# A hybrid decoder block on one core: retention's decay moved into its keys, and the norm work of the heads moved from GpSimd to ScalarE and VectorE

## The chip, the cores and the metric

The kernel runs on one core of one Trainium2 chip. The time is device microseconds of one launch. The core has TensorE (matmuls and transposes), VectorE, ScalarE and GpSimd (elementwise work), and SyncE, whose queue issues nearly all of this kernel's DMAs. In the profile's rows they are PE (PEld is its weight load), DVE, ACT, POOL and SP.

## The reference, cut to what matters

One layer, 512 tokens, model width 1024, everything in float32:

```
h = RMSNorm(x) ;  [q_r,k_r,v_r,g_r, q_f,k_f,v_f,f_f, a_r,a_f] = h @ W_in
y_r = W_ro( silu(g_r) * GroupNorm(Retention(rot(q_r), rot(k_r)/8, v_r)) * g_ret_norm )
y_f = W_fo( ForgettingAttention(RMSNorm(q_f)*g_fox_q, RMSNorm(k_f)*g_fox_k, v_f, log sigmoid(f_f + b)) )
x = x + W_out( sigmoid(a_r)*y_r + sigmoid(a_f)*y_f ) ;  x = x + SwiGLU(RMSNorm(x))

# Retention, 4 heads, keys of 64, values of 128, in chunks of 128 tokens; lg = log of the head's decay
decay[i,j] = exp((i-j)*lg) for i >= j, else 0
out_i   = sum_j (q_i . k_j) decay[i,j] v_j  +  exp((i+1)*lg) * (q_i @ state)
state'  = exp(128*lg) * state + sum_j exp((127-j)*lg) k_j^T v_j
# GroupNorm: per token and head over the 128 values: (o - mean) * rsqrt(var + EPS) * g_ret_norm
```

Forgetting attention has 8 heads of 64; its queries and keys are normed per token and head over their 64 columns.

## The kernel before, in words

Products of float32 are made of three matmuls in the float32r type: a high part (a ScalarE cast, tiles wh, xh) and a low part (a VectorE subtraction, wl, xl) of each operand, high by high, low by high, high by low (`three`, line 179). Weights come in units of 128x1024 (`load_w`, line 152: a DMA into tile raw), are cast on ScalarE (line 162) and subtracted on VectorE (line 163), so each unit needs both engines before TensorE can use it. A 128x512 matmul of these is the kernel's main instruction.

The work goes in stages: the combined projection (first the columns of q_r and k_r into rz, then k, v and gates of retention through sums of blocks of the weights, up to about 62 us), then retention interleaved with the projections of q_f, k_f, v_f and the gates a_r, a_f; then forgetting attention interleaved with the remaining gates and y_r; then the output product, SwiGLU and its down product. The change touches the second stage.

What sets the order: TensorE's order is written out by hand. While `pinned[0]` is true each matmul is chained behind the one before it, and `fill(us)` puts so many microseconds of projection matmuls between the pieces of retention. The order of the DMAs of SyncE (`move`) is chained in the same way. On the other engines a planner orders instructions by when they are ready in its own model, and the code's order breaks ties; `after(a, b)` ties single ones on the same engine. So an instruction may run long before one that the code issues ahead of it.

Retention works chunk by chunk, t from 0 to 3 (loop at line 868):

- `ret_rotate(t)` (line 504), on GpSimd: seven instructions. Products of the two halves of rz with cosine and sine (ta, tb, then tcc, td, 256 columns each), a difference and a sum into rot, and kz, the keys multiplied by their head's zeta = exp((127-j)*lg). For chunk 0 the first of them waits for `last_low`, a VectorE subtraction at the end of the first stage (line 514).
- `ret_square(t)` (line 528): VectorE transposes 32x32 blocks of rot, four DMAs write them to memory; `ret_get(t)` reads them back as rT, with columns along partitions; `ret_keys(t)` copies the keys' half on ScalarE into rK (line 544); `ret_decay(t)` multiplies the queries' half by exp((i+1)*lg) into rX on VectorE (line 549).
- `ret_scores(t)` (line 553): scores on TensorE into two banks tp, multiplied by the decay factors on VectorE into sT (line 561); then kz by values into a bank, and the new state sn (lines 570, 574).
- `ret_values(t)` (line 577): sT by values, and from chunk 1 on rX by state, into two banks sc.
- `ret_norm(t)` (line 590): per head statistics (line 597), a reciprocal root in steps on 128x4 (tiles n4v, n4y, n4a, lines 124 to 132), then og (line 605), all VectorE.
- `ret_out(t)` (line 608): GpSimd multiplies the gate gs by g_ret_norm (line 610); VectorE multiplies og by it (line 611); TensorE transposes og (line 85) into a bank tp; a cast on ScalarE and a subtraction on VectorE (lines 188, 189) make orh and orl.

The projection of q_f has its evacuation in `evac_qf` (line 650: ScalarE for the columns, and in the second half VectorE for the forget gate fz, line 654), that of k_f in `evac_kf`. Behind each evacuated block of tokens `head_norm` squares on ScalarE (line 634) and sums per head on VectorE (line 635); behind the last, a reciprocal root on 128x32 (n8v, n8y, n8a) and then GpSimd multiplies all four blocks by it (line 641), and q_f also by the norm weights (line 643). `turn_heads` transposes 32x32 blocks on VectorE (line 675), and DMAs through memory put heads' columns along partitions, where `fox_prep` (line 700) makes the parts of queries and keys. `turn_q` (line 689) is called twice a chunk and does one step of this for q_f at a time.

Of the kernel before, what the change touches and what calls it, by code (L numbers as in the profile page):

```python
# [17 lines left out]
P = 128  # L18
# [19 lines left out]
C_EARLY = C_GCH + 2  # L38
# [14 lines left out]
def block_kernel(ctx: ExitStack, tc, x, xT, c_early, c_tab, c_late, w_qf, w_tok, w_vg, w_a, w_y, w_o, w_gu, w_gl, w_dn, w_dh, out):  # L53
# [64 lines left out]
    def rsqrt(dst, ss, inv_n, shape, nm, pool=None, behind=None):  # L118
# [5 lines left out]
        first = ts(out=v, in0=ss, scalar1=inv_n, scalar2=EPS, op0=ALU.mult, op1=ALU.add)  # L124
# [210 lines left out]
    def split_to_parts(src, h, l):  # L335
        nc.scalar.copy(out=h, in_=src)
        tt(out=l, in0=src, in1=f32(h), op=ALU.subtract)
# [166 lines left out]
    def ret_rotate(t):  # L504
        z5 = rz[:, t, :].rearrange("p (a h s d) -> p a h s d", a=2, h=RH, s=2)
        z1, z2 = z5[:, :, :, 0, :], z5[:, :, :, 1, :]
        c = cosv[:, t].broadcast_to([P, 2, RH, 32])
        s = sinv[:, t].broadcast_to([P, 2, RH, 32])
        rot = rwk.tile([P, 512], F32, name="rot", tag="rot", bufs=3)
        r5 = rot.rearrange("p (a h s d) -> p a h s d", a=2, h=RH, s=2)  # L510
        ta = rwk.tile([P, 2, RH, 32], F32, name="ta", tag="ta", bufs=1)
        tb = rwk.tile([P, 2, RH, 32], F32, name="tb", tag="tb", bufs=1)
        first = gp.tensor_tensor(out=ta, in0=z1, in1=c, op=ALU.mult)
        if t == 0:
            tc.add_manual_dep(first.ins, last_low.ins.name, mybir.DependencyInfo(mybir.DependencyClass.Sync, mybir.DependencyReason.DATA), reason="GpSimd's part comes behind most of the sums")
        gp.tensor_tensor(out=tb, in0=z2, in1=s, op=ALU.mult)
        gp.tensor_tensor(out=r5[:, :, :, 0, :], in0=ta, in1=tb, op=ALU.subtract)
        td = rwk.tile([P, 2, RH, 32], F32, name="td", tag="ta", bufs=1)
        tcc = rwk.tile([P, 2, RH, 32], F32, name="tcc", tag="tb", bufs=1)
        gp.tensor_tensor(out=tcc, in0=z1, in1=s, op=ALU.mult)  # L520
        gp.tensor_tensor(out=td, in0=z2, in1=c, op=ALU.mult)
        gp.tensor_tensor(out=r5[:, :, :, 1, :], in0=tcc, in1=td, op=ALU.add)
        kz = rwk.tile([P, 256], F32, name="kz", tag="kz", bufs=3)
        last = gp.tensor_tensor(out=kz.rearrange("p (h d) -> p h d", h=RH), in0=rot[:, 256:512].rearrange("p (h d) -> p h d", h=RH),
                         in1=ce[:, C_ZETA:C_ZETA + RH].rearrange("p (h o) -> p h o", o=1).broadcast_to([P, RH, RDK]), op=ALU.mult)
        ret[t].update(rot=rot, kz=kz, rotated=last)
# [15 lines left out]
    def ret_keys(t):  # L542
        rK = rwk.tile([P, 2, P], F32, name="rK", tag="rK")
        nc.scalar.copy(out=rK.rearrange("p a (c i) -> p a c i", i=32), in_=ret[t]["rT"][:, :, 2:4, :].rearrange("p c a i -> p a c i"))
        ret[t].update(rK=rK)

    def ret_decay(t):
        rX = rwk.tile([P, 2, P], F32, name="rX", tag="rX")
        ret[t]["decay"] = tt(out=rX.rearrange("p a (c i) -> p a c i", i=32), in0=ret[t]["rT"][:, :, 0:2, :].rearrange("p c a i -> p a c i"),
           in1=xiT.rearrange("p a (c i) -> p a c i", i=32), op=ALU.mult)  # L550
        ret[t].update(rX=rX)

    def ret_scores(t):
        rT, kz = ret[t]["rT"], ret[t]["kz"]
        sT = rwk.tile([P, 512], F32, name="sT", tag="sT")
        sps = [bank("tp") for e in range(2)]
        for e, sp in enumerate(sps):
            rows = slice(e * 64, (e + 1) * 64)
            for a in range(2):
                mm(sp[:, a * P:(a + 1) * P], lhsT=ret[t]["rK"][rows, a, :], rhs=rT[rows, :, a, :], start=True, stop=True)  # L560
            tt(out=sT[:, e * 256:(e + 1) * 256], in0=sp[:, 0:256], in1=dec[:, e * 256:(e + 1) * 256], op=ALU.mult)
        ret[t].update(sT=sT)
        if t < NT - 1:
# [12 lines left out]

    def ret_values(t):
        rT, sT = ret[t]["rT"], ret[t]["sT"]
# [5 lines left out]
        if t:  # L584
            for e, a, os in pairs:
                rows = slice(e * 64, (e + 1) * 64)
                mm(o[e][:, os], lhsT=ret[t]["rX"][rows, a, :], rhs=ret[t]["st"][rows, a, :], start=False, stop=True, skip_group_check=True)
        ret[t].update(o=o)

    def ret_norm(t):  # L590
# [10 lines left out]
        rsqrt(r4, mv[:, :, 1], 1.0, [P, RH], "n4")  # L601
# [6 lines left out]
    def ret_out(t):  # L608
        og = ret[t]["og"]
        after(gp.tensor_tensor(out=gs[:, t, :], in0=gs[:, t, :], in1=gret, op=ALU.mult), ret[2]["rotated"])  # L610
# [5 lines left out]
        ret[t]["split"] = split_ps(pt.rearrange("p (h q) -> p h q", h=RH), orh[:, :, tq], orl[:, :, tq])  # L616
# [9 lines left out]
    gp.tensor_tensor(out=gqk, in0=gqk, in1=cl[:, C_GQK + FD:C_LATE], op=ALU.mult)  # L626

    def head_norm(z, g=None):
# [3 lines left out]
        def one(t):  # L632
# [3 lines left out]
            if t == NT - 1:  # L636
                r8 = sm.tile([P, NT, FH], F32, name="r8", tag="r8")
                rsqrt(r8.rearrange("p t h -> p (t h)"), s8.rearrange("p t h -> p (t h)"), 1.0 / FD, [P, NT * FH], "n8", behind=ret[0].get("normed"))
                for u in range(NT):
                    z3 = z[:, u, :].rearrange("p (h d) -> p h d", h=FH)  # L640
                    gp.tensor_tensor(out=z3, in0=z3, in1=r8[:, u, :].rearrange("p (h o) -> p h o", o=1).broadcast_to([P, FH, FD]), op=ALU.mult)
                    if g is not None:
                        gp.tensor_tensor(out=z3, in0=z3, in1=g.rearrange("p (o d) -> p o d", o=1).broadcast_to([P, FH, FD]), op=ALU.mult)
                normed.append(z)
# [3 lines left out]
    qnorm, knorm = head_norm(qf, gqk), head_norm(kf)  # L648

    def evac_qf(t, c, acc):  # L650
        sc = rstd1[:, t:t + 1]
        act(out=qf[:, t, c * 256:c * 256 + 256], in_=acc[:, 0:256], func=AF.Copy, scale=sc)
        if c:
            fox["fz"] = stt(out=fz[:, t, :], in0=acc[:, 256:264], scalar=sc, in1=ce[:, C_BF:C_BF + FH], op0=ALU.mult, op1=ALU.add)  # L654
            qnorm(t)

    def evac_kf(t, c, acc):
        act(out=kf[:, t, :], in_=acc, func=AF.Copy, scale=rstd1[:, t:t + 1])
        knorm(t)
# [10 lines left out]
    def turn_heads(z, ts_=range(NT)):  # L670
# [189 lines left out]
    move(rd1, rt)  # L860
    ret_rotate(2)
# [4 lines left out]
    ret_decay(0)  # L866
    ret_square(1)
    for t in range(NT):
        if t == 1:
            ret_rotate(t + 2)  # L870
# [13 lines left out]
        if t + 1 < NT:  # L884
            ret_decay(t + 1)
# [587 lines left out]
def _constants():  # L1473
# [8 lines left out]
    def rope(a):  # L1482
        a = a.astype(f).reshape(NT, P, half).transpose(1, 0, 2)
        return np.stack([a, a * f(RDK ** -0.5)], 2).reshape(P, NT * 2 * half)

    diff = idx[None, :] - idx[:, None]
    dec = [np.where(diff >= 0, ex(np.maximum(diff, 0) * lg[h]), 0).astype(f) for h in range(RH)]
    xi = np.stack([np.concatenate([np.tile(ex((idx + f(1)) * lg[2 * a + e]), (RDK, 1)) for e in range(2)]) for a in range(2)], 1).reshape(P, 2 * P)
    zeta = np.stack([ex((f(P - 1) - idx) * lg[h]) for h in range(RH)], 1)
    gch = ex(f(P) * lg)  # L1490
# [4 lines left out]
        "ident": np.eye(P, dtype=f), "xi": xi, "zeta": zeta, "gch": gchp, "tri": tri, "mask": mask,  # L1495
        "cos": rope(np.cos(ang)), "sin": rope(np.sin(ang)), "dec": np.concatenate([dec[0], dec[2], dec[1], dec[3]], 1),
# [7 lines left out]
def _layout(i):  # L1504
# [5 lines left out]
        _CONST["zeta"], _CONST["gch"]], 1)  # L1510
# [63 lines left out]
```

## Time and profile before

| | |
|---|---|
| median of 3 runs | 689.62 us (687.66, 689.62 and 1730.48) |
| profiled execution, own time | 689.82 us |
| its span, first to last instruction | 688.0 us |
| TensorE busy | 674.8 us (98%) |
| VectorE busy | 541.3 us (79%) |
| ScalarE busy | 350.5 us (51%) |
| GpSimd busy | 76.3 us (11%) |
| granted TensorE clock, mean | 0.997 |

A row of a timeline gives start, duration, engine, line, operation, tile written, tiles read, shapes and count; in brackets stands the idle time before it on its engine and what ended that. A matmul's duration is modelled to its end and overlaps the next one: the pace is read from the starts. A row by group gives busy time, mean nanoseconds of one, and the idle time before. Lines are those of the kernel; 82 and 85 are the helpers for all matmuls and all transposes, so tiles tell them apart. In the rows of forgetting attention, pT is its transposed weights.

### The profile page before, as it was taken

How to read it: one execution, taken by the hardware profiler on the slowest of the kernel's cores; microseconds unless marked ns; L12 is line 12 of the kernel's file. 1: busy time of each engine (PE TensorE's matmuls, PEld its weight loads, DVE VectorE, ACT ScalarE, POOL GpSimd, SP SyncE). 2: the span in 40 equal slices, each digit the busy share in tenths (PEclk: the TensorE clock that was granted, in tenths of full speed). 3: DMA queues.
4: the chain of work that ended last, by engine and by line, in shares of the span. 5: the costliest groups of instructions: out<-in, count | busy, mean ns of one | idle time of the engine just before them, and what ended most of it. 6: DMA issues, size and time to landing. Idle time of an engine off the chain costs nothing.

```text
span 688.0 us, 9396 instructions
## 1 busy us (share of the span) xinstructions
PE 674.8 (98%) x3375; PEld 562.8 (82%) x3375; DVE 541.3 (79%) x869; ACT 350.5 (51%) x515; POOL 76.3 (11%) x97
## 2 busy tenths in 40 slices
PE   8999998999999999999999999999999999999998
PEld 6877976888887777788888888888888898888997
DVE  6899489875768684576979998989989888756794
ACT  6667353431546444554656655564646474443341
POOL 0013946010212210000230000000000000000000
PEclk9999999999999999999999999999999999999999
DMA  8910543525638878526710614536362522644221
GB/s 271 421 51 32 153 141 93 193 84 185 199 96 243 221 224 255 175 92 236 283 61 1 244 32 146 150 113 183 86 180 52 124 101 61 160 143 159 81 103 62
DMA packets 85806, 101.30 MB, mean 147 GB/s; under 512 B 52960, under 2 KB 62336, under 8 KB 84992
## 3 DMA queue, kind: packets, MB, share of 16 engines
q1 hardware_dynamic: 84976, 99.64, 46.1%
q10 hardware_dynamic: 784, 1.06, 0.6%
q8 instruction: 26, 0.43, 0.3%
q14 instruction: 20, 0.16, 0.1%
HBM read 83.28 MB, written 10.58 MB: 136 GB/s over the span
## 4 chain that ended last, share of the span: by engine, by line
PE 62%; DVE 2%; DMA 2%; ACT 1%; issue 1%; SPq 0%; POOL 0%; DVEq 0%; ACTq 0%
PE acc L82 47%; PE sc L82 11%; PE tp L82 4%; DMA pd<-psq 1%; DVE ps L1073 1%; DMA pT<-pd 1%; ACT ps L1072 1%; DMA b<-in_w_gl_dram 0%; DVE psq L752 0%; DVE b L1081 0%; SPq L72 0%; DVE wl L163 0%; DVE us L1275 0%; DVE us L1270 0%; ACT wh L162 0%
## 5 line engine op out<-in xcount | busy, mean ns | idle before, releaser
L82 PE MATMUL acc<-ps,xfh 128*128 128x512 f32 (+1 forms) x576 | 166.7, 372 | 0.3 <-ACT us L1194 0.3
L82 PEld LDWEIGHTS acc<-ps,xfh 128*128 128x128 f32 x576 | 105.2, 188 | 19.2 <-ACT us L1194 0.5
L1072 ACT CAST ps<-b 128x1024 fp32r<-128x1024 f32 (+1 forms) x84 | 82.4, 981 | 60.4 <-PE acc L82 26.9
L1073 DVE TENSOR_TENSOR ps<-b,ps 128x1024 fp32r<-128x1024 f32 (+1 forms) x84 | 94.4, 1135 | 18.9 <-ACT ps L1072 17.7
L82 PE MATMUL acc<-ps,xfl 128*128 128x512 f32 (+1 forms) x288 | 106.9, 371 | 0.0
L162 ACT CAST wh<-raw 128x1024 fp32r<-128x1024 f32 (+1 forms) x44 | 46.1, 1050 | 96.0 <-PE acc L82 47.2
L163 DVE TENSOR_TENSOR wl<-raw,wh 128x1024 fp32r<-128x1024 f32 (+1 forms) x44 | 57.4, 1306 | 30.9 <-ACT wh L162 30.9
L82 PEld LDWEIGHTS acc<-ps,xfl 128*128 128x128 f32 x288 | 54.3, 188 | 9.2
L82 PE MATMUL acc<-wh,xh 128*128 128x512 f32 (+2 forms) x144 | 50.6, 351 | 1.5 <-DVE fz L654 1.5
L1081 DVE TENSOR_TENSOR b<-b,b 128x1024 f32<-128x1024 f32 (+1 forms) x48 | 52.1, 1125 | 0.0
L82 PE MATMUL acc<-xh,wh 128*128 128x512 f32 x128 | 50.8, 397 | 0.0
L82 PE MATMUL acc<-xh,wl 128*128 128x512 f32 x128 | 50.3, 393 | 0.0
L82 PE MATMUL acc<-xl,wh 128*128 128x512 f32 x128 | 50.1, 392 | 0.0
L82 PE MATMUL acc<-wh,xl 128*128 128x512 f32 (+2 forms) x144 | 50.0, 347 | 0.0
L82 PE MATMUL acc<-wl,xh 128*128 128x512 f32 (+2 forms) x144 | 49.9, 347 | 0.0
L82 PE MATMUL acc<-hl,ps 128*128 128x512 f32 x168 | 40.4, 389 | 0.0
L82 PEld LDWEIGHTS acc<-hl,ps 128*128 128x128 f32 x168 | 31.5, 188 | 6.5
L1194 ACT COPY us<-acc 128x512 f32<-128x512 f32 (+1 forms) x48 | 26.1, 551 | 16.2 <-PE acc L82 15.3
L82 PEld LDWEIGHTS acc<-wh,xh 128*128 128x128 f32 x144 | 27.6, 192 | 5.5 <-DVE fz L654 1.8
L1120 DVE TENSOR_TENSOR ps<-raw,ps 128x1024 fp32r<-128x1024 f32 x14 | 17.1, 1219 | 18.8 <-ACT ps L1117 18.8
L740 ACT ACTIVATE pr<-pr,nm 128x512 f32<-128x512 f32 (+3 forms) x32 | 18.0, 563 | 24.4 <-DVE nm L738 24.0
L82 PEld LDWEIGHTS acc<-wh,xl 128*128 128x128 f32 x144 | 27.6, 192 | 3.4
(296 smaller groups left out, 1447.3 us busy)
## 6 DMA issues: line engine op xcount, KB each, us to landing
b<-in_w_gu_dram SPq DMA_DIRECT2D x40, 512.0 KB, 4.7
raw<-in_w_a_dram SPq DMA_DIRECT2D x16, 512.0 KB, 4.5
raw<-in_w_dn_dram SPq DMA_DIRECT2D x14, 512.0 KB, 3.9
pd<-psq SPq DMA_DIRECT2D x8, 640.0 KB, 6.7
pT<-pd SPq DMA_DIRECT2D x32, 160.0 KB, 3.4
pf<-squares SPq DMA_DIRECT2D x160, 32.0 KB, 1.9
blk<-in_w_vg_dram SPq DMA_DIRECT2D x8, 512.0 KB, 10.4
raw<-in_w_tok_dram SPq DMA_DIRECT2D x8, 512.0 KB, 3.9
```

What stands on the lines that cost most here:

```text
L82: in_order(nc.tensor.matmul(o, **kw))
L162: split_raw.last = (nc.scalar.copy(out=h[:, :width], in_=raw[:, :width]), tt(out=l[:, :width], in0=raw[:, :width], in1=f32(h)[:, :width], ...
L163: tt(out=l[:, :width], in0=raw[:, :width], in1=f32(h)[:, :width], op=ALU.subtract))
L740: fox["last"] = act(out=pr[:, :n], in_=pr[:, :n], func=AF.Exp, scale=-1.0, bias=nm, accum_out=fox["rs", a][:, e, i:i + 1])
L1072: part.cast = nc.scalar.copy(out=h, in_=raw)
L1073: low = tt(out=l, in0=raw, in1=f32(h), op=ALU.subtract)
L1081: queue(tt(out=raws[g][b][v], in0=raws[g][b][v], in1=raws[g][c][v], op=ALU.add))
L1120: tt(out=l, in0=raw, in1=f32(h), op=ALU.subtract)
L1194: copy = nc.scalar.copy(out=u_(tp, slot), in_=os[tp][:, :w])
```

## The change

- **Decay into the keys.** The scores are (q_i . k_j) exp((i-j)*lg). The change multiplies key j by exp((127-j)*lg)/8 before the rotation and leaves the factor exp((i-127)*lg) of each query's row out altogether: it is the same for the whole row of a head, GroupNorm divides it out, and only EPS has to be scaled, by exp(2*(127-i)*lg). So the decay factors become a plain causal mask (`tri`, ones above the diagonal), rX, kz and their tables go, the rotated keys serve both products, and the state is multiplied by exp(128*lg) after the addition instead of before it.
- **Rotation.** Four passes of ScalarE over 128x64 multiply each head's key columns of rz in place. GpSimd then needs four instructions: all 512 columns by cosine, all by sine, a difference and a sum of 256 columns each. The key copy of `ret_keys` now covers queries too (128x512).
- **g_ret_norm** is applied after the transposes, where it is a column: four ScalarE passes over 128x128 from the bank back into og; the cast and the subtraction then read og. GpSimd's product with the gate goes.
- **Head norms.** VectorE multiplies q_f and k_f by their reciprocal roots in `turn_heads`, just ahead of each block's transpose. The norm weights of q_f and k_f, a column once the heads are turned, are applied by four ScalarE passes over 128x512 (gcol). Squares and sums come behind the last evacuation of each projection, and q_f's reciprocal root and multiplies come behind the split of chunk 0.
- **Order.** `ret_square(1)` comes earlier, ahead of `ret_rotate(2)`; `ret_rotate(3)` moves ahead of the loop; the tie points of the 32x32 transposes change.

TensorE's matmuls are the same in number and order.

```diff
     def ret_rotate(t):
-        z5 = rz[:, t, :].rearrange("p (a h s d) -> p a h s d", a=2, h=RH, s=2)
-        z1, z2 = z5[:, :, :, 0, :], z5[:, :, :, 1, :]
...
+        z3 = rz[:, t, :].rearrange("p (g d) -> p g d", d=32)
         rot = rwk.tile([P, 512], F32, name="rot", tag="rot", bufs=3)
...
-        first = gp.tensor_tensor(out=ta, in0=z1, in1=c, op=ALU.mult)
+        for h in range(RH):
+            hs = slice(256 + h * RDK, 256 + (h + 1) * RDK)
+            act(out=rz[:, t, hs], in_=rz[:, t, hs], func=AF.Copy, scale=ce[:, C_ZETA + h:C_ZETA + h + 1])
...
+        first = gp.tensor_tensor(out=ta, in0=z3, in1=cosv[:, t].broadcast_to([P, 16, 32]), op=ALU.mult)
...
-        gp.tensor_tensor(out=tb, in0=z2, in1=s, op=ALU.mult)
-        gp.tensor_tensor(out=r5[:, :, :, 0, :], in0=ta, in1=tb, op=ALU.subtract)
...
-        gp.tensor_tensor(out=tcc, in0=z1, in1=s, op=ALU.mult)
-        gp.tensor_tensor(out=td, in0=z2, in1=c, op=ALU.mult)
-        gp.tensor_tensor(out=r5[:, :, :, 1, :], in0=tcc, in1=td, op=ALU.add)
-        kz = rwk.tile([P, 256], F32, name="kz", tag="kz", bufs=3)
-        last = gp.tensor_tensor(out=kz..., in0=rot[:, 256:512]..., in1=ce[:, C_ZETA:C_ZETA + RH]..., op=ALU.mult)
+        gp.tensor_tensor(out=tb, in0=z3, in1=sinv[:, t].broadcast_to([P, 16, 32]), op=ALU.mult)
+        r4, a4, b4 = (f.rearrange("p (g s) d -> p g s d", s=2) for f in (rot.rearrange("p (g d) -> p g d", d=32), ta, tb))
+        gp.tensor_tensor(out=r4[:, :, 0, :], in0=a4[:, :, 0, :], in1=b4[:, :, 1, :], op=ALU.subtract)
+        last = gp.tensor_tensor(out=r4[:, :, 1, :], in0=a4[:, :, 1, :], in1=b4[:, :, 0, :], op=ALU.add)

     def ret_square(t):
-        after(one, (turn_of[0], ret[0].get("decay"), ret[1].get("new"), ret[0].get("out"))[t])
+        after(one, (turn_of[0], split_raw.last[1], ret[0].get("scored"), ret[0].get("out"))[t])

     def ret_keys(t):
-        rK = rwk.tile([P, 2, P], F32, name="rK", tag="rK")
-        nc.scalar.copy(out=rK..., in_=ret[t]["rT"][:, :, 2:4, :]...)
+        rK = rwk.tile([P, 4, P], F32, name="rK", tag="rK")
+        nc.scalar.copy(out=rK..., in_=ret[t]["rT"]...)

-    def ret_decay(t):
...
     def ret_scores(t):
...
-            tt(out=sT[:, e * 256:(e + 1) * 256], in0=sp[:, 0:256], in1=dec[:, e * 256:(e + 1) * 256], op=ALU.mult)
+            ret[t]["scored"] = tt(out=sT[...]..., in0=sp[:, 0:256]..., in1=causal, op=ALU.mult)
...
-                    new = stt(out=sn[:, a, :], in0=st[:, a, :], scalar=ce[:, C_GCH + a:C_GCH + a + 1], in1=kv[...], op0=ALU.mult, op1=ALU.add)
+                    nc.vector.tensor_tensor_reduce(out=sn[:, a, :], in0=ret[t]["st"][:, a, :], in1=kv[:, a, :], scale=ce[:, C_GCH + a:C_GCH + a + 1],
+                                                   scalar=3e38, op0=ALU.add, op1=ALU.min, accum_out=junk[:, a:a + 1])

     def ret_out(t):
-        after(gp.tensor_tensor(out=gs[:, t, :], in0=gs[:, t, :], in1=gret, op=ALU.mult), ret[2]["rotated"])
         ret[t]["out"] = tt(out=og, in0=og, in1=gs[:, t, :], op=ALU.mult)
...
-        ret[t]["split"] = split_ps(pt.rearrange("p (h q) -> p h q", h=RH), orh[:, :, tq], orl[:, :, tq])
+        for h in range(RH):
+            act(out=og[:, h * P:(h + 1) * P], in_=pt[:, h * P:(h + 1) * P], func=AF.Copy, scale=ce[:, C_GRET + h:C_GRET + h + 1])
+        ret[t]["split"] = split_to_parts(og.rearrange("p (h q) -> p h q", h=RH), orh[:, :, tq], orl[:, :, tq])

+    gsq = sm.tile([P, 32], F32, name="gsq", tag="gsq", bufs=1)
+    for c in range(4):
+        gp.tensor_copy(out=gsq[32 * c:32 * c + 32], in_=gqk[32 * c:32 * c + 32, c % 2 * 32:c % 2 * 32 + 32])

-    def head_norm(z, g=None):
+    def head_norm(z, late=False):
...
-                rsqrt(r8..., s8..., 1.0 / FD, [P, NT * FH], "n8", behind=ret[0].get("normed"))
-                for u in range(NT):
-                    gp.tensor_tensor(out=z3, in0=z3, in1=r8[:, u, :]..., op=ALU.mult)
-                    if g is not None:
-                        gp.tensor_tensor(out=z3, in0=z3, in1=g..., op=ALU.mult)
+                normed.append(finish)
+                if not late:
+                    finish()
+
+        def finish():
+            fox["r8"] = sm.tile([P, NT, FH], F32, name="r8", tag="r8")
+            rsqrt(fox["r8"]..., s8..., 1.0 / FD, [P, NT * FH], "n8")

     def evac_qf(t, c, acc):
...
-            qnorm(t)
+            if t == NT - 1:
+                for u in range(NT):
+                    qnorm(u)

     def turn_heads(z, ts_=range(NT)):
...
-            one = nc.vector.transpose(...)
+            one = tt(out=z3, in0=z3, in1=fox["r8"][:, t, :]..., op=ALU.mult)
+            after(one, ret[0]["split"])
+            nc.vector.transpose(...)

     def turn_q():
-        if normed and "rotated" in ret[NT - 1]:
+        if normed and "split" in ret[0]:
...
+            elif n == 4:
+                for c in range(4):
+                    act(out=qf[:, c, :], in_=qf[:, c, :], func=AF.Copy, scale=gcol[:, 0:1])

     move(rd1, rt)
+    nc.vector.transpose(out=gcol, in_=gsq)
+    ret_square(1)
     ret_rotate(2)
...
     ret_scores(0)
-    ret_decay(0)
-    ret_square(1)
+    ret_rotate(3)
     for t in range(NT):
-        if t == 1:
-            ret_rotate(t + 2)
...
-            ret_decay(t + 1)
             ret_keys(t + 1)
```

More of the change, by code (lines that the diff above doesn't have):

```diff
@@ L123, in rsqrt @@
         y = yi.bitcast(F32)
-        first = ts(out=v, in0=ss, scalar1=inv_n, scalar2=EPS, op0=ALU.mult, op1=ALU.add)
+        if eps is None:
+            first = ts(out=v, in0=ss, scalar1=inv_n, scalar2=EPS, op0=ALU.mult, op1=ALU.add)
+        else:
+            first = tt(out=v, in0=ss, in1=eps, op=ALU.add)
         if behind is not None:
@@ L336, in split_to_parts @@
         nc.scalar.copy(out=h, in_=src)
-        tt(out=l, in0=src, in1=f32(h), op=ALU.subtract)
+        return tt(out=l, in0=src, in1=f32(h), op=ALU.subtract)
     def x_block(b):
@@ L542, in ret_keys @@
     def ret_keys(t):
-        rK = rwk.tile([P, 2, P], F32, name="rK", tag="rK")
-        nc.scalar.copy(out=rK.rearrange("p a (c i) -> p a c i", i=32), in_=ret[t]["rT"][:, :, 2:4, :].rearrange("p c a i -> p a c i"))
+        rK = rwk.tile([P, 4, P], F32, name="rK", tag="rK")
+        nc.scalar.copy(out=rK.rearrange("p a (c i) -> p a c i", i=32), in_=ret[t]["rT"].rearrange("p c a i -> p a c i"))
         ret[t].update(rK=rK)
-    def ret_decay(t):
[L548 to L551, printed above, removed]
     def ret_scores(t):
-        rT, kz = ret[t]["rT"], ret[t]["kz"]
+        rT, kh = ret[t]["rK"], ret[t]["rot"][:, 256:512]
         sT = rwk.tile([P, 512], F32, name="sT", tag="sT")
@@ L559, in ret_scores @@
             for a in range(2):
-                mm(sp[:, a * P:(a + 1) * P], lhsT=ret[t]["rK"][rows, a, :], rhs=rT[rows, :, a, :], start=True, stop=True)
-            tt(out=sT[:, e * 256:(e + 1) * 256], in0=sp[:, 0:256], in1=dec[:, e * 256:(e + 1) * 256], op=ALU.mult)
+                mm(sp[:, a * P:(a + 1) * P], lhsT=rT[rows, 2 + a, :], rhs=rT[rows, a, :], start=True, stop=True)
+            ret[t]["scored"] = tt(out=sT[:, e * 256:(e + 1) * 256].rearrange("p (a q) -> p a q", a=2), in0=sp[:, 0:256].rearrange("p (a q) -> p a q", a=2), in1=causal, op=ALU.mult)
         ret[t].update(sT=sT)
@@ L674, in turn_heads @@
         for t in ts_:
-            one = nc.vector.transpose(out=turn_heads.sq.rearrange("p b a t j -> p a b t j")[:, :, :, t, :], in_=z[:, t, :].rearrange("p (a b j) -> p a b j", a=4, b=4))
-            if "split" in ret[0]:
-                after(one, ret[0]["split"])
+            z3 = z[:, t, :].rearrange("p (h d) -> p h d", h=FH)
+            one = tt(out=z3, in0=z3, in1=fox["r8"][:, t, :].rearrange("p (h o) -> p h o", o=1).broadcast_to([P, FH, FD]), op=ALU.mult)
+            after(one, ret[0]["split"])
+            nc.vector.transpose(out=turn_heads.sq.rearrange("p b a t j -> p a b t j")[:, :, :, t, :], in_=z[:, t, :].rearrange("p (a b j) -> p a b j", a=4, b=4))
     def put_heads(z, sq, name):
@@ L1482, in rope @@
     def rope(a):
[L1483 to L1488, printed above, removed]
+        return a.astype(f).reshape(NT, P, half).transpose(1, 0, 2).reshape(P, NT * half)
     zeta = np.stack([ex((f(P - 1) - idx) * lg[h]) for h in range(RH)], 1)
+    eps = np.stack([ex((f(P - 1) - idx) * (f(2) * lg[h])) for h in range(RH)], 1) * f(EPS)
     gch = ex(f(P) * lg)
```

89 lines of the change are left out of this document (39 added, 50 removed).

## The prediction

> **What bounds the kernel now.** I read the page first, then the busy time by stretch, then the timelines of TensorE, VectorE, GpSimd and ScalarE around the stretches in which TensorE is not full.
>
> ```profile
> span 688.0 us, 9396 instructions
> PE 674.8 (98%) x3375; PEld 562.8 (82%) x3375; DVE 541.3 (79%) x869; ACT 350.5 (51%) x515; POOL 76.3 (11%) x97
> ```
>
> TensorE is busy for 674.8 of 688.0 us, so all that a change outside TensorE can win is 13.2 us less what start and end need. The profiled execution took 689.82 us (1.8 around the span); the median of the runs is 689.62, so a sum made against 689.82 holds for the median within 0.2. The change touches retention and the head norms. Their stretch, with TensorE, its weight loads, VectorE, ScalarE and GpSimd busy in each piece, then the granted clock:
>
> ```profile
> 92.00:95.00 3.00, 1.58 (x7) 1.32 (x8) 3.00 (x7) 2.48 (x5) 1.70 (x2) 1.00 0.69 208
> ...
> 104.00:109.00 5.00, 5.00 (x23) 3.80 (x21) 4.83 (x14) 1.06 (x1) 4.08 (x4) 1.00 0.00 0
> ...
> 112.00:117.00 5.00, 4.89 (x17) 3.97 (x18) 5.00 (x7) 3.38 (x4) 3.38 (x2) 0.66 0.51 116
> ```
>
> From 92 to 95 TensorE is busy for 1.58 of 3, and from 112 to 117 it has a clock of 0.66, both times beside a full VectorE and a busy GpSimd. Its rows:
>
> ```profile
> 91.59 0.28 PE L82 MATMUL acc<-wh,xl 128*128 128x264 f32 x1
> 93.42 0.50 PE L82 MATMUL acc<-wh,xh 128*128 128x512 f32 x1 [1.55 <-DVE fz L654]
> ...
> 108.39 0.39 PE L82 MATMUL acc<-wl,xh 128*128 128x512 f32 x1
> 108.62 0.39 PE L82 MATMUL acc<-wh,xl 128*128 128x512 f32 x1
> 112.11 0.63 PE L85 MATMUL tp<-ctab,og 128*128 128x128 f32 x4 [3.11 <-issue]
> 112.50 0.48 PE L82 MATMUL acc<-wh,xh 128*128 128x512 f32 x1
> ...
> 116.93 0.39 PE L82 MATMUL acc<-wh,xh 128*128 128x512 f32 x1
> ```
>
> Undisturbed, a 128x512 matmul starts 0.23 after the one before. Wait B: 93.42 less 91.59, less the 0.12 of a 264-column matmul, is 1.71 lost. Wait C: 112.11 less 108.62, less 0.23, is 3.26 lost; then twelve matmuls take 116.93 - 112.50 = 4.43 instead of 12 x 0.227 = 2.72, another 1.71 at the low clock. Together 6.68 us.
>
> What B and C wait for stands on VectorE, and what holds VectorE on GpSimd:
>
> ```profile
> 87.32 2.24 DVE L163 TENSOR_TENSOR wl<-raw,wh 128x1024 fp32r<-128x1024 f32 x1 [5.41 <-ACT wh L162]
> ...
> 90.92 2.31 DVE L163 TENSOR_TENSOR wl<-raw,wh 128x1024 fp32r<-128x1024 f32 x1
> 93.15 0.35 DVE L654 SCALAR_TENSOR_TENSOR fz<-acc,rstd,ce 128x8 f32<-128x8 f32 x2
> ...
> 99.58 0.29 DVE L597 BATCH_NORM_STATS2 bs<-sc 128x6 f32<-128x128 f32 x1
> ...
> 102.79 1.22 DVE L163 TENSOR_TENSOR wl<-raw,wh 128x1024 fp32r<-128x1024 f32 x1
> 104.89 0.16 DVE L131 TENSOR_TENSOR n4a<-n4a,n4v 128x4 f32<-128x4 f32 x1
> ...
> 107.02 1.22 DVE L131 TENSOR_TENSOR n4a<-n4a,n4v 128x4 f32<-128x4 f32 x1
> ...
> 110.99 1.02 DVE L611 TENSOR_TENSOR og<-og,gs 128x512 f32<-128x512 f32 x1
> ```
> ```profile
> 87.20 4.95 POOL L610 TENSOR_TENSOR gs<-gs,cl 128x512 f32<-128x512 f32 x3
> ...
> 104.92 2.06 POOL L641 TENSOR_TENSOR qf<-qf,r 128x512 f32<-128x512 f32 x2 [11.22 <-issue]
> ```
>
> The same wl subtraction takes 2.24 and 2.31 us while GpSimd multiplies gs, 1.22 when GpSimd rests. A 128x4 step of the reciprocal root takes 0.16 at 104.89 and, the same line, 1.22 at 107.02, once GpSimd's qf multiplies have begun at 104.92: it waits out about one GpSimd instruction.
>
> **The change, part by part.**
>
> *Gate factors and the last rotation leave GpSimd's 82 to 94.* The four L610 are gone, and a rotation of a chunk has four GpSimd instructions instead of seven, with 512 columns in two of them. Rows for these and for ScalarE's:
>
> ```profile
> 61.98 0.74 POOL L513 TENSOR_TENSOR ta<-rz,cl 128x256 f32<-128x256 f32 x1 [18.16 <-DVE wl L163]
> ```
> ```profile
> L641 POOL TENSOR_TENSOR qf<-qf,r 128x512 f32<-128x512 f32 x4 | 4.1, 1044 | 11.2 <-issue 11.2
> L517 POOL TENSOR_TENSOR rot<-ta,tb 128x256 f32<-128x256 f32 x4 | 3.0, 742 | 0.2
> L652 ACT ACTIVATE qf<-acc,rstd 128x256 f32<-128x256 f32 x8 | 3.2, 472 | 1.9 <-PE acc L82 1.9
> L307 ACT ACTIVATE vf<-acc,rstd 128x512 f32<-128x512 f32 x4 | 2.7, 690 | 2.4 <-PE acc L82 2.4
> ```
>
> By the means in ns, two at 1.04 and two at 0.74 make 3.6 us a chunk. The first may begin at 62, behind a VectorE low that the code has it wait for; four chunks are through by 62 + 14.4 = 76. Only the end of chunk 3 waits for a rot buffer, which chunk 0's key product, right behind its scores (at 79, row below), frees; so GpSimd rests from about 82. Then the two wl from 87.32 on take 1.22 each, rX between them is gone, and VectorE is free at about 89.8: fz comes when its bank is done, not at 93.15. B falls from 1.71 to 0 (bounds 0 and 1.71; I take 0, since VectorE is then 3.3 us earlier and 1.7 are needed).
>
> *Head norms go from GpSimd to VectorE.* With the qf multiplies gone from 104.92, the steps stay at 0.16 to 0.2. Also the 32-column reciprocal root of qf, which shared VectorE with chunk 0's own root, comes behind chunk 0's split. For the new length of the chain from the first statistics to the gated product I take chunk 2, which has two wl between its steps:
>
> ```profile
> 141.68 0.46 DVE L597 BATCH_NORM_STATS2 bs<-sc 128x6 f32<-128x128 f32 x2
> 149.44 0.69 DVE L611 TENSOR_TENSOR og<-og,gs 128x512 f32<-128x512 f32 x1
> ```
>
> 149.44 + 0.69 - 141.68 = 8.45, against 112.01 - 99.58 = 12.43 in chunk 0. Begun 1.71 earlier than now, at 97.9, it ends at 106.3; the transposes' turn, also 1.71 earlier, is 108.85 - 1.71 = 107.1. C falls to 0, and with it the low clock. Bounds: 0, and 0.9 of wait if the statistics begin as late as now; a wait this short has no low clock behind it (the 1.55 of B had none).
>
> The cover of the eight multiplies on VectorE (8 x 0.69 = 5.5 us by L611) is slack. Those of qf, and the moved root of 12 steps (0.16 each by 104.89), fall between chunk 0's split and chunk 1's gated product, 4 x 0.69 + 1.9 = 4.7 us more ahead of
>
> ```profile
> 130.26 0.68 DVE L611 TENSOR_TENSOR og<-og,gs 128x512 f32<-128x512 f32 x1
> 133.49 0.60 PE L85 MATMUL tp<-ctab,og 128*128 128x128 f32 x4
> ```
>
> which has 133.49 - 130.94 = 2.55 in hand. Bounds 0 and 4.7 - 2.55 = 2.1. I take 0: from 112 to 117 VectorE's 5.00 of 5 was partly waiting beside GpSimd's 3.38, rX goes, and kf's squares, which stood among chunk 1's steps, now come behind the last evacuation. The kf multiplies take the place of VectorE's waits for GpSimd's, 0.
>
> *ScalarE takes over the columns.* A pass over 128x64 is, on the line through 472 and 690 ns, about 0.31; 16 make 5.0 us. The 16 passes over transposed 128x128 blocks (0.36 each) put 1.4 us ahead of each chunk's split, the larger key copy is 0.28 more (four times), the q columns 4 x 0.69. All lie on an engine that is busy half of the time; the split of the retained heads is first read by the y products, tens of us later. Price 0 there. Where the 16 narrow passes fall is the open question:
>
> ```profile
> 40.00:50.00 10.00, 10.00 (x45) 7.99 (x43) 9.39 (x20) 6.76 (x10) 0.97 (x1) 1.00 0.00 0
> 50.00:60.00 10.00, 9.23 (x40) 7.20 (x40) 9.96 (x11) 6.54 (x8) 0.00 (x0) 1.00 0.01 2
> ```
> ```profile
> 42.86 0.97 POOL L516 TENSOR_TENSOR tb<-rz,cl 128x256 f32<-128x256 f32 x1 [4.14 <-ACT rz L307]
> ```
> ```profile
> 43.14 1.83 DVE L413 TENSOR_TENSOR sums<-xf 128x512 f32<-128x512 f32 x2
> ...
> 64.55 1.27 DVE L477 TENSOR_TENSOR gs<-acc,u 128x512 f32<-128x512 f32 x2
> ```
>
> tb of chunk 0 ran at 42.86, 19 us ahead of the ta that the code issues before it: engines take what is ready in the order that the planner found, not the order of the code. ScalarE's gaps from 40 to 60 are 3.24 + 3.46 = 6.7 us, and the 5.0 fit. But from 50 to 60 TensorE follows the chain of block sums, casts and lows with no slack (9.23 of 10 busy, VectorE 9.96). tb, now 512 wide, moves from 42.9 behind its chunk's column passes, to 47 or later, and can hold a VectorE step by up to its own 1.04 (at 43.14 two sums took 1.83 beside tb's 0.97, 0.55 more than the two L477 of the same size). Bounds: -0.8 (these waits go) to +1.6 (a hold of 1.04 and two narrow passes ahead of a cast). I take +0.7, the hold that the row shows and half a pass. The Trainium skill, page "SBUF — State Buffer", section "Who interferes with whom", speaks against this edit: VectorE with two SBUF inputs and a GpSimd instruction that reads SBUF exclude each other, and the second waits out the whole of the first. The wl rows bear that out (2.24 for 1.22); by the rule at its full length the sum below would be 0.5 higher, 684.3, by the row at 43.14 it is as given.
>
> *The rest* is like for like: causal factors for decay factors, two state updates of the same shape, two columns more in ce, less of c_late. No matmul is added or removed, TensorE's order is the pinned one.
>
> Sum: -1.71 - 4.97 + 0.7 = -5.98; 689.82 - 5.98 = **683.8 us**.
>
> **The rivals.**
>
> *Slower: the first scores are late.* If the planner puts chunk 0's column passes behind the gates and casts with which ScalarE is busy up to 71.8, rotation 0 ends at 71.8 + 1.0 + 3.6 = 76.4, not 67.1.
>
> ```profile
> 66.01 1.07 POOL L522 TENSOR_TENSOR rot<-tcc,td 128x256 f32<-128x256 f32 x1
> ```
> ```profile
> 69.77 2.01 ACT L162 CAST wh<-raw 128x1024 fp32r<-128x1024 f32 x2
> ...
> 77.67 0.41 ACT L544 COPY rK<-rT 128x256 f32<-128x256 f32 x1 [0.51 <-DMA rT<-zr]
> ```
> ```profile
> 79.11 0.72 PE L82 MATMUL tp<-rT,rK 64*128 64x128 f32 x8
> ```
>
> From 67.08 to the end of rK at 78.08 are 11.0 us of transpose, write, read and copy; 76.4 + 11.0 + 0.28 = 87.7, TensorE wants it at 79.11: 8.6 waited and 1.7 of low clock, 683.8 + 10.3 = 694. It begins to cost when these passes end after about 64.2 (the rotation behind them takes 3.6, the copies leave 0.7), and eats the whole gain at 68.5 (4.3 and the low clock). For it: the passes stand last in the code, and ScalarE is full from 62 on. Against: rz of chunk 0 is there when tb starts at 42.86, and that early start itself.
>
> *Moved, not removed.* VectorE's new work holds chunk 0's or chunk 1's gated product: a wait of 2.1 us (the bound above) at 107 or 127, with or without 1.7 of low clock. 683.8 + 2.1 to 683.8 + 3.8: 686 to 688. For: VectorE is at 4.83 of 5 and 5.00 of 5 there. Against: the 2.55 in hand. On the low clock, the Trainium skill, page "TensorE: Matmul & The Clock Gate", section "What's actually happening", has it come after an idle window of about 3.4 us; the trace has 1.00 behind 1.55 us of idling and 0.66 behind 3.11. By the page this rival would stay at 686.
>
> *Given back later.* Forgetting attention's chain (heads through memory) does not come earlier with TensorE, and TensorE waits there for 6 us more: 689.8. For: in the list of waits TensorE stands for that chain's pT twice, its only waits after the transposes. Against: the chain starts from TensorE's own products, so it moves with them.
>
> **How the numbers follow.** Forecast 0.62 (681.5 to 686), moved 0.14, given back 0.10, late scores 0.11, more than forecast 0.03. The range runs from 681.0 (B and C gone, the 0.77 between 50 and 60 too, 1.4 of difference between runs) to 690.5, given back with as much, which leaves out late scores and tails; the likeliest's own is 681.5 to 686. About 2%, 13.8 us, is what a measurement of this kernel can tell from no change. Faster than that would take every idle us of TensorE: 0.02. Slower by it, over 703, needs late scores and a second wait: 0.05. Within: 0.93.
>
> **What would show it.** Right: no TensorE wait at 92 and 107, clock 1.00 behind it; 128x4 steps at 0.16 to 0.2 throughout; GpSimd's busy time down by some 30 from 76.3; column passes of all chunks before 60; chunk 0's gated product done by 107. Wrong: a wait ahead of the first scores at 79, a tail of VectorE steps over 0.9 with GpSimd active, or TensorE waits over 2 us from 120 on. Any of these wrong alone leaves the forecast off by its own price; all of B and C still there would mean that GpSimd was not what held VectorE.

## The result, and the profile after

The changed kernel takes 693.65 us (median of 10 runs, 692.12 to 697.1), the kernel before 689.3 beside it: ratio 1.0069, interval 1.0049 to 1.009. One of the ten runs of the kernel before took 1730.48 us and is left out of the ratio. The change is slower by 0.7%, where 683.8 was predicted, and outside the range of 681.0 to 690.5. The prediction held 2% for the least that a measurement can tell from no change; here the interval shows a difference of 0.7%. The profiled execution took 692.4 us; its page, and the three stretches that showed the stalls before (TensorE, its weight loads, VectorE, ScalarE, GpSimd, then the granted clock):

```profile
span 690.6 us, 9419 instructions
...
PE 682.4 (99%) x3375; PEld 562.3 (81%) x3375; DVE 536.1 (78%) x878; ACT 362.3 (52%) x551; POOL 53.5 (8%) x73
```
```profile
92.00:95.00 3.00, 3.00 (x23) 2.87 (x22) 1.11 (x4) 1.80 (x5) 0.00 (x0) 1.00 1.00 300
104.00:109.00 5.00, 5.00 (x23) 4.03 (x22) 4.93 (x19) 1.14 (x2) 0.00 (x0) 1.00 0.00 0
112.00:117.00 5.00, 5.00 (x37) 4.25 (x36) 3.85 (x9) 2.60 (x4) 0.00 (x0) 1.00 0.78 261
```

TensorE is now busy all through the stretches in which it stood, at a clock of 1.00, and GpSimd does nothing there: waits B and C are gone. Yet the span grew by 2.6 us, and the busy time of TensorE by 7.6 us, with the same 3375 matmuls. So the loss is not a wait. Its timeline shows what it is. First the kernel before, then the one after, the first and the last row of one undisturbed run of 128x512 matmuls, all one behind the other:

```profile
19.79 0.39 PE L82 MATMUL sc<-wh,xh 128*128 128x512 f32 x1
...
29.99 0.39 PE L82 MATMUL acc<-wh,xh 128*128 128x512 f32 x1
```
```profile
19.65 0.39 PE L81 MATMUL tp<-wh,xl 128*128 128x512 f32 x1
...
29.92 0.39 PE L81 MATMUL acc<-wh,xl 128*128 128x512 f32 x1
```

Before, 45 matmuls start in 10.20 us, 0.2267 each; after, 44 in 10.27, 0.2334 each. The durations in the rows (0.39) are modelled and tell nothing of it; starts and counts do. Another view of the same, 140 us of SwiGLU in which TensorE is full in both, before and after:

```profile
400.00:540.00 140.00, 140.00 (x620) 115.95 (x619) 127.68 (x131) 81.45 (x98) 0.00 (x0) 1.00 0.44 119
```
```profile
400.00:540.00 140.00, 140.00 (x609) 114.12 (x608) 126.11 (x130) 80.50 (x97) 0.00 (x0) 1.00 0.45 118
```

609 instructions instead of 620 at the same clock, in a stage whose code the change does not touch.

To see where the time went, I cut the timeline of TensorE at three rows that all kernels have: the last 264-column matmul of the query projection, the transposes of chunk 3, and the last matmul. Before, and after:

```profile
91.59 0.28 PE L82 MATMUL acc<-wh,xl 128*128 128x264 f32 x1
...
171.17 0.60 PE L85 MATMUL tp<-ctab,og 128*128 128x128 f32 x4
...
684.63 0.28 PE L82 MATMUL sc<-xfh,c 128*128 128x256 f32 x1
```
```profile
93.99 0.28 PE L81 MATMUL acc<-wh,xl 128*128 128x264 f32 x1
...
168.37 0.60 PE L84 MATMUL tp<-ctab,og 128*128 128x128 f32 x4
...
687.18 0.28 PE L81 MATMUL sc<-xfh,c 128*128 128x256 f32 x1
```

Front: 2.40 lost. Middle: 79.58 before, 74.38 after, 5.20 won. Rest: 513.46 before, 518.81 after, 5.35 lost.

### The profile page after: what moved, and what is told of

The parts are those of the page before. It is cut to its first block, busy times and chain, and to the rows that moved or that the text cites. A ratio compares the mean times of both kernels' runs of the same rounds, so it can differ in the third digit from the quotient of the medians.

```text
span 690.6 us, 9419 instructions
## 1 busy us (share of the span) xinstructions
PE 682.4 (99%) x3375; PEld 562.3 (81%) x3375; DVE 536.1 (78%) x878; ACT 362.3 (52%) x551; POOL 53.5 (8%) x73
## 4 chain that ended last, share of the span: by engine, by line
PE 64%; DMA 3%; DVE 1%; ACT 1%; SPq 0%; issue 0%; DVEq 0%; ACTq 0%
PE acc L81 49%; PE sc L81 11%; PE tp L81 4%; DMA pT<-pd 1%; DMA pd<-psq 1%; DMA tk<-tk 1%; SPq L71 0%; ACT ps L1073 0%; DVE ps L1074 0%; DVE b L1082 0%; ACT us L1236 0%; DVE us L1286 0%; DVE hl L1130 0%; DVE us L1235 0%; DVE pf L1460 0%
## 5 line engine op out<-in xcount | busy, mean ns | idle before, releaser
L165 DVE TENSOR_TENSOR wl<-raw,wh 128x1024 fp32r<-128x1024 f32 (+1 forms) x44 | 55.0, 1251 | 36.4 <-ACT wh L164 36.4
L81 PEld LDWEIGHTS acc<-wl,xh 128*128 128x128 f32 x144 | 27.2, 189 | 3.6
```

The source lines that it names most:

```text
L81: in_order(nc.tensor.matmul(o, **kw))
L165: tt(out=l[:, :width], in0=raw[:, :width], in1=f32(h)[:, :width], op=ALU.subtract))
```

## The experiments

The pace changed from the first matmuls on, in stages whose code is the same, so I looked for something that all matmuls share. The change adds tiles: `ce` has 38 columns instead of 30 (its 120 bytes grow to 152; rounded up to multiples of 32 that is 128 and 160, 32 more), and the pool `sm`, on the other side of the buffer, gains gsq, gcol and two of junk (128 + 128 + 64 = 320 bytes). The pools are stacked from both ends, so every operand on the left side (weights wh, wl) starts 32 bytes higher in each partition and every one on the right side (xh, xl, sums sh, sl, the inputs xfh, xfl) 320 bytes lower. Before, two unused tiles made each of them start at a multiple of 256:

```python
PAD_CST, PAD_FTOK, PAD_SM = 107, 104, 16
...
    cst.tile([P, PAD_CST], F32, name="pad")
    sm.tile([P, PAD_SM], F32, name="pad", tag="pad", bufs=1)
```

The change leaves these as they are. My theory (where the expectations use letters, A, with a number for a variant): the start addresses of the operands set the pace. Its rivals: (B) the new instructions on VectorE and ScalarE slow the matmuls beside them; (C) the executions of the change ran at a slower clock of the chip. (These letters are not the waits B and C.) For the vanished waits the theory (D) is that GpSimd held VectorE; the rival (E), that VectorE's own queue, with two roots and the sums of squares mixed, made chunk 0's product late, so that the new order of the steps did it.

**The change with its operands at multiples of 256 again** (label a_al), all instructions as in the change:

```diff
-PAD_CST, PAD_FTOK, PAD_SM = 107, 104, 16
+PAD_CST, PAD_FTOK, PAD_SM = 99, 104, 64
```

> The changed kernel with two pad tiles resized (107 to 99 columns on the left side of SBUF, 16 to 64 on the right), so that every matmul operand starts at a multiple of 256 bytes again, as before the change; in the change the constants tile ce grew by 32 bytes and small tiles by 320, which moved all that lies behind them. Theory A, the addresses: the 128x512 matmuls start every 0.227 us again instead of 0.233, and the time is 682 to 685 us. Theory B, the change's own work on VectorE and ScalarE slows TensorE's reads: the pace stays 0.233 and the time 692 to 694. Theory C, the executions of the changed kernel ran at a slower chip clock: no difference on the same chip, 692 to 694, or kernel before and this both slower.

It took 685.86 us (684.17 to 686.14) beside 689.8: ratio 0.9929, 0.9903 to 0.9955. Only the length of two unused tiles is different, and 7.8 us are back (693.65 less 685.86; each was measured beside the kernel before). Its pace and its three cuts:

```profile
400.00:540.00 140.00, 140.00 (x619) 116.00 (x618) 127.69 (x133) 80.82 (x98) 0.00 (x0) 1.00 0.45 123
```
```profile
93.87 0.28 PE L81 MATMUL acc<-wh,xl 128*128 128x264 f32 x1
...
166.71 0.60 PE L84 MATMUL tp<-ctab,og 128*128 128x128 f32 x4
...
680.93 0.28 PE L81 MATMUL sc<-xfh,c 128*128 128x256 f32 x1
```

**The kernel before, with its operands where the change has them** (label b_sh). The instructions are those of before, one for one:

```diff
-PAD_CST, PAD_FTOK, PAD_SM = 107, 104, 16
+PAD_CST, PAD_FTOK, PAD_SM = 115, 104, 96
```

> The kernel before, with nothing but its two pad tiles enlarged (107 to 115 columns, 16 to 96), so that its operands start where the changed kernel has them (32 bytes past a multiple of 256 on the left side, 64 short of one on the right). The instructions and their order are the same. Theory A: pace 0.233, and 9 to 11 us more, 698 to 701 us. Theories B and C: 689 us, pace 0.227.

697.5 us (696.13 to 699.51), ratio 1.0107, 1.0073 to 1.0142, and the pace of the change (233.3 and 234.0 ns in the table below). With the run before it, this splits the result: instructions -3.9 (685.86 less 689.8), addresses +7.7 (697.5 less 689.8), sum +3.8; measured +4.35. Both rivals fall: no new instruction runs here, and on the same chip, beside these runs, the kernel before took 689.8. Both times lie just outside what was expected, a_al 0.9 over and b_sh 0.5 under; the paces are those of theory A.

**One side at a time** (labels b_left, left side 32 bytes up, PAD_CST 115; b_right, right side 320 bytes down, PAD_SM 96), in the kernel before:

> The kernel before with the left side alone moved by 32 bytes (pad of 115 columns). Theory A1, an operand at 32 past a multiple of 64 bytes costs, and one at 192 past a multiple of 256 does not: all of the loss of the moved kernel, 698 to 701 us, and a pace of 0.233 in every stage in which an operand lies on the left. Theory A2, anything off a multiple of 256 costs: a part of the loss, 693 to 697. Under B and C 689.

> The kernel before with the right side alone moved by 320 bytes (pad of 96 columns), to 192 past a multiple of 256, which is a multiple of 64. Theory A1: no loss, 689 us, pace 0.227. Theory A2: the other part of the loss, 693 to 697 us. Under B and C 689.

b_left 698.42 us (ratio 1.0117, 1.0089 to 1.0145), b_right 695.64 (1.008, 1.0056 to 1.0105). Beside 689.8 the left side alone costs 8.6 us, the right side alone 5.8 and both together 7.7, so the costs do not add. Neither variant fits: A1 has no loss for b_right, and A2 has less for b_left. And in b_right the pace depends on the stage: 228.9 ns from 32 to 62 us, where the moving operand is a weight on the left, 232.4 from 262 to 320, where it is a feature tile on the right.

**By how much must a side be moved** (labels b_left64, b_left128, b_right128: PAD_CST 123, PAD_CST 139, PAD_SM 48), one execution each:

> The kernel before with the left side moved by 64 bytes (pad of 123 columns). Read is the pace of the 128x512 matmuls up to 320 us: 0.227 in the kernel before, 0.233 with the left side moved by 32 bytes, and with the right side at 192 past a multiple of 256, 0.229 where the right holds the stationary operand and 0.2325 where it holds the moving one. Theory A3, only multiples of 256 are free: 0.233 again, some 698 us. Theory A4, multiples of 64 are free for the left side: 0.227 and 690.

> The kernel before with the left side moved by 128 bytes (pad of 139 columns). Theory A3, only multiples of 256 are free: a pace of 0.229 to 0.233. Theory A5, multiples of 128 are free: 0.227 and 690 us.

> The kernel before with the right side moved by 128 bytes (pad of 48 columns). Theory A3: a pace of 0.2325 where the right holds the moving operand (gates, 262 to 320 us). Theory A5: 0.227 there and everywhere, 690 us.

693.74, 696.58 and 695.92 us beside 690.23. Multiples of 64 and of 128 are not free. But b_left64 has the paces of b_right to 0.1 ns, and b_left128 those of b_right128 within 0.3, though it is the other side that lies off. That does not fit a rule for each operand by itself, and led to the next two.

**Both sides off by 128, and one side off by 256** (labels b_both128, PAD_CST 139 and PAD_SM 48; b_left256, PAD_CST 171):

> The kernel before with both pads 32 floats longer: what lies on the left of the buffer moves up by 128 bytes, what lies on the right moves down by 128 bytes, so each operand starts 128 bytes past a multiple of 256 and the distance of any two is a multiple of 256 again. The instructions are the same. If each operand for itself has to start at a multiple of 256, the 128x512 matmul stays at 232 ns from start to start as in the two runs with one side moved by 128, and the time is 695 to 697. If it is the distance between the two operands of one matmul that counts, the matmul is back at 227 ns and the time at 689 to 691.

> The kernel before with the left pad 64 floats longer: what lies on the left moves up by 256 bytes, and every operand starts at a multiple of 256 as before. Under either theory of the start addresses (a multiple of 256 for each, or for their distance) nothing changes: 227 ns and 689 to 691. If any move of the buffers from where the kernel before has them costs, whatever its size, it is 693 to 698.

690.96 and 688.75 us, one execution each, beside 689.55. With one side off by 128, and with both:

```profile
400.00:540.00 140.00, 140.00 (x613) 114.72 (x612) 126.81 (x131) 79.63 (x97) 0.00 (x0) 1.00 0.43 117
```
```profile
400.00:540.00 140.00, 140.00 (x620) 115.95 (x619) 128.32 (x132) 80.45 (x97) 0.00 (x0) 1.00 0.43 118
```

None of the wide operands in the second starts at a multiple of 256, and the pace is that of before. So the theory in its first form, a multiple of 256 for each, falls too: what counts is the distance between the starts of the two operands of one matmul. All eleven kernels agree. Distance is the start of the moving operand less that of the stationary one, modulo 256 bytes; pace is the mean from start to start of 128x512 matmuls, in ns, with the waits left out:

| kernel | distance, pace at 32 to 62 us | distance, pace at 262 to 320 us | median us |
|---|---|---|---|
| before | 0, 227.6 | 0, 226.9 | 689.3 |
| a_al | 0, 226.9 | 0, 226.9 | 685.86 |
| b_both128 | 0, 227.1 | 0, 226.8 | 690.96 |
| b_left256 | 0, 226.7 | 0, 226.8 | 688.75 |
| b_left64 | 64, 228.9 | 192, 232.4 | 693.74 |
| b_right | 64, 228.9 | 192, 232.4 | 695.64 |
| b_left128 | 128, 232.5 | 128, 232.4 | 696.58 |
| b_right128 | 128, 232.6 | 128, 232.1 | 695.92 |
| b_left | 32, 233.3 | 224, 232.8 | 698.42 |
| b_sh | 96, 233.3 | 160, 234.0 | 697.5 |
| after | 96, 233.5 | 160, 233.1 | 693.65 |

The three kernels still to come, all at distance 0, have 226.8 to 227.6.

From 320 us on part of SwiGLU's weights lie on the same side as the inputs; those keep their distance under any pad, and from 400 to 540 us less was lost (620 to 609, 1.8%, against 2.7% from 226.9 to 233.1).

**GpSimd's multiplies taken out** (label b_nogp): the kernel before without lines 610, 641 and 643, so that the norm weight of retention and the norm scaling of q_f and k_f are missing from the result.

```diff
-        after(gp.tensor_tensor(out=gs[:, t, :], in0=gs[:, t, :], in1=gret, op=ALU.mult), ret[2]["rotated"])
...
-                for u in range(NT):
...
-                    gp.tensor_tensor(out=z3, in0=z3, in1=r8[:, u, :]..., op=ALU.mult)
-                    if g is not None:
-                        gp.tensor_tensor(out=z3, in0=z3, in1=g..., op=ALU.mult)
```

> The kernel before without GpSimd's products of the gates with their norm weights and of queries and keys with their reciprocal roots and norm weights: this work is left out, not moved, so the norms of the heads are missing from what is computed. Addresses are as before. Theory D, GpSimd's work held VectorE and so TensorE at 92 and 109: both waits and the low clock behind them go, 682 to 685 us, and the 128x4 steps of chunk 0 take 0.2 us. Rival E, VectorE's own queue (two roots and the sums of squares mixed) made chunk 0's product late: the wait at 109 stays above 1.5 us with its low clock, 687 to 690.

683.63 us (ratio 0.9904, 0.9879 to 0.9929). Rotation, rX and the old order stay, and B and C go: theory D holds, rival E falls. The two wl behind which fz had waited, 2.24 and 2.31 us before (neither reads anything that GpSimd's products write):

```profile
87.16 1.23 DVE L163 TENSOR_TENSOR wl<-raw,wh 128x1024 fp32r<-128x1024 f32 x1 [5.48 <-ACT wh L162]
88.30 0.42 DVE L549 TENSOR_TENSOR rX<-rT,cl 128x256 f32<-128x256 f32 x1
88.64 1.22 DVE L163 TENSOR_TENSOR wl<-raw,wh 128x1024 fp32r<-128x1024 f32 x1
```

TensorE at the two places, where the matmul in front started at 91.68 and at 106.88, and the step on 128x4 that had taken 1.22:

```profile
91.80 0.40 PE L82 MATMUL acc<-wh,xh 128*128 128x512 f32 x1
...
107.11 0.60 PE L85 MATMUL tp<-ctab,og 128*128 128x128 f32 x4
```
```profile
104.34 0.16 DVE L131 TENSOR_TENSOR n4a<-n4a,n4v 128x4 f32<-128x4 f32 x1
```

**A version that beats both.** Three waits of TensorE are left at the front of a_al:

```profile
53.46 0.50 PE L81 MATMUL acc<-wh,sh 128*128 128x512 f32 x1 [0.63 <-ACT wh L164]
54.72 0.50 PE L81 MATMUL acc<-wl,sh 128*128 128x512 f32 x1 [0.53 <-DVE wl L165]
...
80.84 0.39 PE L81 MATMUL acc<-wh,xh 128*128 128x264 f32 x1 [0.99 <-ACT qf L645]
```

v_get moves one request ahead, v_both ties one GpSimd instruction as well:

```diff
     ret_square(0)
+    ret_get(0)
     fill(RF[0])
...
-    ret_get(0)
```
```diff
-        gp.tensor_tensor(out=tb, in0=z3, in1=sinv[:, t].broadcast_to([P, 16, 32]), op=ALU.mult)
+        second = gp.tensor_tensor(out=tb, in0=z3, in1=sinv[:, t].broadcast_to([P, 16, 32]), op=ALU.mult)
+        after(second, first)
```

> The realigned change (pads 99 and 64) with the request for the transposed rotary rows of chunk 0 issued right after the squares of that chunk, ahead of the load of the next raw weights on SP's queue. If the wait of TensorE at 80.8 us for the evacuations of the query (0.99 us) is the late transposed key row, passed on by ScalarE's order, it goes and the time is about 684.8 (685.86 less 1.0). If the row comes no earlier, or ScalarE has another reason to be late, the wait stays and the time is 685.5 to 686.

> As the run before, and in the rotation the wide product with the sines is tied behind the one with the cosines, so that the two do not hold VectorE one after the other at 49 to 52 us in another order. If the waits of TensorE at 53.5 and 54.7 us (0.63 and 0.53) come from VectorE and ScalarE held by that product, half of them go: about 684.3. If the product is held at the same place anyway, the time equals the run before. Against the kernel before (about 689.6) the ratio is expected at 0.992 to 0.993, against the realigned change at 0.998.

v_get took 686.14 us (0.9939, 0.9918 to 0.996): my reading of the wait at 80.8 was wrong. The key copy now runs 3.7 us earlier (76.07 for 79.80), and the wait is still there. ScalarE:

```profile
76.07 0.62 ACT L537 COPY rK<-rT 128x512 f32<-128x512 f32 x1 [2.67 <-DMA rT<-zr]
80.23 1.07 ACT L164 CAST wh<-raw 128x1056 fp32r<-128x1056 f32 x1 [3.54 <-DMA raw<-in_w_qf_dram]
```

What is ahead of the query's evacuations is the cast of the next weights, and it waits for their load, which now stands behind the request on SP's queue. v_both took 684.01 us (682.91 to 685.16; 0.9915, 0.9897 to 0.9934). In the profile all three waits are gone; in time the intervals of a_al, v_get and v_both overlap, so only that each beats the kernel before, and with it the change as it came, is measured. VectorE's product of blocks, first in the change, where tb(0) ran beside it, then in v_both, where GpSimd rests until 62:

```profile
49.69 2.31 DVE L409 TENSOR_TENSOR blk<-blk,blk 128x1024 f32<-128x1024 f32 x1
```
```profile
50.93 1.22 DVE L409 TENSOR_TENSOR blk<-blk,blk 128x1024 f32<-128x1024 f32 x1
```

In v_both the load is asked for at 73.34 (74.68 in v_get), its cast runs at 77.05, and the wait at 80 is gone as well. That this follows from the hold is read from one profile of each, not tested. Why the load itself took 3.7 us here and 5.5 there was not tried.

## Why the prediction was wrong, point by point

**The step that failed** is *The rest is like for like*. It gave the paragraph no price, because no matmul is added or removed and their order is pinned. That reason is true, and the matmuls still became slower, by the place of their operands, which it did not look at. The term was put at 0 and is 7.8 us (693.65 less 685.86), more than the whole forecast gain of 6. Without it the change takes 685.86 us (a_al): inside the range, 2 us over the forecast. The paragraph also counted "two columns more in ce" where there are eight. Two would have fitted into the 128 bytes that `ce` takes anyway, but the new small tiles on the right, which it does not name, were enough by themselves (b_right: 5.8 us).

**B and C: right, mechanism and size, but for one detail.** Both were put at 0, with the low clock, 6.68 us together. With the pace as before, the middle section takes 166.71 - 93.87 = 72.84 us instead of 79.58: 6.74 won, and the same 72.84 in v_both. In the change itself 1.54 of it is eaten by the pace. The steps on 128x4 that had taken 1.22 beside GpSimd take 0.16, and chunk 0's gated product ends at 108.40, 1.33 ahead of its transposes' turn at 109.73 (not 106.3, since everything is later by the front and the pace):

```profile
105.04 0.15 DVE L132 SCALAR_TENSOR_TENSOR n4a<-n4y 128x4 f32<-128x4 f32 x1
105.11 0.18 DVE L133 TENSOR_TENSOR n8a<-n8a,n8v 128x32 f32<-128x32 f32 x1
105.22 0.16 DVE L133 TENSOR_TENSOR n4a<-n4a,n4v 128x4 f32<-128x4 f32 x1
...
107.71 0.69 DVE L599 TENSOR_TENSOR og<-og,gs 128x512 f32<-128x512 f32 x1
```

The detail is the row of n8a: the prediction, and the account of the change, had the 32-column root of q_f come behind chunk 0's split, but in the change its steps still run between those of chunk 0, from 102.42 to 106.11. The code issues them later, yet ties only the multiplies behind the split, and the planner left the root where it was. So the forecast of C did not need that step: C went with both roots mixed. That GpSimd is what had held VectorE is shown by b_nogp; what the later squares and sums add was not tried.

**The front: right place, too small.** I took +0.7. a_al loses 2.28 up to the last 264-column matmul (v_both 0.84): 0.39 more of waits at 50 to 55 (1.16 for 0.77), 0.99 at 80.84, which I had not priced, and 0.9 by 28.2 us, where the first group of weights is through. That start differs from one execution to the next: with the instructions of before and the pace of before it came at 27.27 (before), 28.04 (b_both128) and 29.95 (b_left256), so the 0.9 can't be put down to the change. The hold by tb(0) was read at 0.55 from the row at 43.14; it measured 2.31 - 1.22 = 1.09:

```profile
48.91 2.01 POOL L515 TENSOR_TENSOR tb<-rz,cl 128x512 f32<-128x512 f32 x1 [9.64 <-ACT rz L509]
```

The Trainium skill, page "SBUF — State Buffer", section "Who interferes with whom", has the second of two such instructions wait out the whole of the first. The rows agree: VectorE's product, which took 1.22 where GpSimd rested, begins at 49.69 and ends at 52.00, 1.08 after tb(0) has ended at 50.92. The rule at its full length, for which the prediction had 1.04, was the better guide.

**GpSimd's busy time** fell to 53.5, not to about 46. In the rows by group the wide products cost 1.38 and 1.83 us, not 1.04:

```profile
L515 POOL TENSOR_TENSOR tb<-rz,cl 128x512 f32<-128x512 f32 x4 | 7.3, 1834 | 9.6 <-ACT rz L509 9.6
L512 POOL TENSOR_TENSOR ta<-rz,cl 128x512 f32<-128x512 f32 x4 | 5.5, 1384 | 11.9 <-DVE wl L165 11.7
```

The shortest of them, with its broadcast table, took 1.3 us, the longest 2.3, and the four copies that make gsq, which were not counted, took 2.6 together. That the longer ones wait on VectorE, as VectorE waits on them, is read from the rows: tb(0), 2.01 us long, began at 48.91, while VectorE's wl ran from 48.55 to 49.77.

**The rivals.** *The first scores are late*: not so, the column passes of all chunks ran between 46.7 and 56.5, as forecast. Its milder relative is the 0.99 at 80.84. *Moved, not removed*: no wait at chunk 1's transposes (129.84). *Given back later*: a part. TensorE's waits for pT are 3.29 us in a_al, 2.42 before; 0.87 of the gain is returned there. So for a_al: -6.74 + 2.28 + 0.76 (the rest, 514.22 instead of 513.46) = -3.70, the difference of the last matmuls, 680.93 and 684.63. None of the rivals, and no case in the range, had the matmul itself change its pace.

## What to carry to other kernels

A tile added anywhere moves all that is stacked behind it. Where a kernel has unused tiles that only take room, treat their lengths as part of the tuning, and set them again when any tile changes. If TensorE's busy time grows while its instruction count does not, compare starts and counts in a stretch without waits before looking for a stall.

## What the runs showed of the hardware that was not expected

- In this kernel the pace of a float32r 128x512 matmul goes with the distance of its two operands' start addresses: 226.7 to 227.6 ns at a multiple of 256 bytes, 228.9 at 64, about 232.4 at 128 and 192, 232.8 to 234.0 at the distances that are no multiple of 64 (32, 96, 160, 224). Of 64 and 192 each was seen in one of the two stages alone. Both operands may lie off by the same 128 at no cost (b_both128). The Trainium skill, page "SBUF — State Buffer", section "Who interferes with whom", calls the read ports for the moving operand and for the weights independent; by that alone no such distance would matter, and the runs decide. What in the memory makes it so was not tried.
- In the shorter matmuls between 62 and 92 us the effect is small or absent. With the waits left out, those of 264 columns start every 120.9 to 121.1 ns at distance 0 and every 121.6 to 122.6 at the others, those of 256 columns every 119.8 to 119.9 at distance 0 and every 116.7 to 120.0 at the others, so there it is no slower.
